# Score matmuls of two head pairs issued as one run of 24 on four PSUM banks

## The chip, the cores and the metric

One Trainium2 chip, one NeuronCore. The metric is the device time of the kernel in microseconds (us); lower is better. The engines that matter are TensorE (PE for its matmuls, PEld for its weight loads), VectorE (DVE), ScalarE (ACT), GpSimd (POOL) and SyncE (SP, whose queue starts most transfers).

## The reference

With DEPTH = 1 only the attention layer runs, then the final norm. S = 256 tokens, D = 1024, 16 heads of 64; the block of keys is 256 long, so every query attends causally inside the one block and nothing is gathered.

```
h = rms_norm(x, norm_g)
q, k, v, gate = split(h @ w_in, 4)
s_own = einsum('bhqd,bhld->bhql', q_c, k_own) * dh ** -0.5
s_own = s_own - slopes * (t_f[:, None] - pos_own[None, :])
s_own = where(pos_own[None, :] <= t_int[:, None], s_own, -inf)
p = softmax(s_own)
o = einsum('bhql,bhld->bhqd', p, v_own)
x = x + (o * silu(gate)) @ w_out
return rms_norm(x, final_norm_g)
```

## The kernel before

All matmuls work on fp32r operands that are split into a high and a low part, so that each product is three matmuls: high by high, high by low and low by high (lines 582, 650, 672). A weight piece of 128x1024 arrives by DMA as `w`, ACT copies it to `whi` (split_hi, line 230) and DVE subtracts to get `wlo` (split_lo, line 243); whi and wlo have four buffers each (NW), w has four (NL). split_lo also starts the next load on the SP queue.

The projections run part by part in the order of PARTS (line 28): v0 q0 k0 g0 q1 k1 g1 q2 k2 v1 q3 k3 g2 g3, each part accumulating in two of the eight PSUM banks (line 638). A q or k part j gives the transposed q or k of head pairs 2j and 2j+1. At a part's end `evac` (line 455) adds a small generator, a fiber, that scales the bank into z, splits it into hi and lo (qh, ql, kh, kl; lines 491 to 497) and, for a k part, adds a second fiber, `fiber_pair`, for each of the two pairs.

`fiber_pair(p)` (line 322) does the attention of heads 2p and 2p+1. It waits for q and k of its pair, takes two PSUM banks (one for each head), and issues 12 score matmuls (lines 344 to 349): for the second half of the queries (m = 1, 256 keys) and then for the first half (m = 0, 128 keys), three products, each for two heads. A head has 64 contraction rows, so the two heads use the upper and the lower 64 rows of the array and run as two at a time. Then DVE adds the ALiBi bias and takes the row extremes (line 365), ACT takes the exponentials with their sums (line 369), the rows are normalized (lines 375 to 389), TensorE transposes them (six transposes of 128x128, line 403, in `tr`, line 111), ACT and DVE split the transposed blocks into pth and ptl (lines 409 and 411), TensorE multiplies with v (lines 429 and 432), and cs, og, oh and ol (lines 437 to 453) give the output projection its operand: oh and ol of pair p are its k-step p.

The order of all queues is written out in advance. The program keeps a planner's clock for each engine (class Plan, line 64) and issues an instruction when the planner's time says that its inputs are there. After each projection matmul it calls `fill()`, which places weight splits by their due times, and `side()` (line 297), which lets the first ready fiber take one step up to its next `yield 0`. `poll()` looks again 50 ns later by the planner's clock. `take(keep)` (line 128) gives a bank only when more than `keep` banks are free; keep[0] is 2 during the projections, so that a pair takes its banks when four are free. `stage["s"]` counts the pairs whose scores are issued, `stage["t"]` those whose transposes are, and SWITCH = 100 ns is what the planner adds before and after each run of scores.

The output projection (line 670) uses five banks; k-steps 0 to 3 go through all of them, 15 matmuls each, and k-steps 4 to 7 then finish bank after bank (line 696), each finished bank going to the residual sum and the final norm (lines 700 to 718) and out.

Of the kernel before, what the change touches and what calls it, by code (L numbers as in the profile page):

```python
# [13 lines left out]
P = 128  # L14
S = 256
D = 1024
H = 16
DH = 64
# [30 lines left out]
NPR = 3  # L49
# [11 lines left out]
SWITCH = 100.0  # L61
# [26 lines left out]
def trunk(ctx: ExitStack, tc, laid, fin_g, out):  # L88
    nc = tc.nc
    plan = Plan()  # L90
# [37 lines left out]
    def take(keep):  # L128

        av = [b for b in banks if not b["busy"] and b["free"] <= plan.pe]  # L130
        if len(av) <= keep:
            return None
        b = min(av, key=lambda b: b["free"])
        b["busy"] = True
        return b

    def take_now():
        b = min((b for b in banks if not b["busy"]), key=lambda b: b["free"])
        b["busy"] = True
        return b  # L140
# [149 lines left out]
    at_q, at_k, at_v, at_g, at_o = {}, {}, {}, {}, {}  # L290
    qs, ks = {}, {}
    stage = {"s": 0, "t": 0, "v": 0, "e": 0}
    keep = [2]
# [25 lines left out]
    def poll():  # L319
        return plan.pe + 50.0  # L320

    def fiber_pair(p):
        while p not in at_k or p not in at_q:
            yield poll()
        qh, ql = qs[p]
        kh, kl = ks[p]
        yield max(at_k[p], at_q[p])
        while stage["s"] < p or stage["t"] < p - NPR + 1:
            yield poll()
        while True:  # L330
            b0 = take(keep[0] + 1)
            if b0 is not None:
                break
            yield poll()
        bs = [b0, take_now()]
        st = sp.tile([P, 2, P + S], F32, name="st")
        pr = sp.tile([P, 2, P + S], F32, name="pr")
        mx = sm.tile([P, 4], F32, name="mx")
        rs = sm.tile([P, 4], F32, name="rs")
        ri = sm.tile([P, 4], F32, name="ri")  # L340

        plan.pe += SWITCH
        at_s = {}
        for m, c in ((1, slice(0, S)), (0, slice(S, S + P))):
            for jj, (u, w) in enumerate(((qh, kh), (qh, kl), (ql, kh))):
                for a in range(2):
                    rr = slice(a * DH, (a + 1) * DH)
                    nc.tensor.matmul(bs[a]["t"][:, c], u[rr, m * P:(m + 1) * P], w[rr, 0:c.stop - c.start],  # L348
                                     start=jj == 0, stop=jj == 2)
                at_s[m] = plan.mm(c.stop - c.start)  # L350
        plan.pe += SWITCH
        stage["s"] = p + 1
        r = at_s[0]
        yield 0
        for m in (1, 0):
# [70 lines left out]
        for a in range(2):  # L426
            w = [vv[m][:, 2 * p + a].rearrange("p t n -> p (t n)") for m in range(NM)]
# [13 lines left out]
        for a in range(2):  # L441
            rr = slice(a * DH, (a + 1) * DH)
# [12 lines left out]
    def evac(kind, j, f, b, r):  # L455
        fibers.insert(0, [0.0, fiber_evac(kind, j, f, b, r)])
        if kind == "k":
            fibers.append([0.0, fiber_pair(2 * j + f)])
# [45 lines left out]
    with tc.manual_schedule():  # L504
# [132 lines left out]
        for kind, j in PARTS[1:]:  # L637
            acc = [take_now() for _ in range(2)]
            dep = [b["free"] for b in acc]
            w = CW if kind == "v" else GW  # L640
            kp = KP * GW // w
            for k in range(NK):
# [5 lines left out]
                for f in range(2):  # L648
                    fs = slice(f * P, (f + 1) * P)
                    for jj, (xx, ww) in enumerate(((xh, whi), (xl, whi), (xh, wlo))):  # L650
                        if kind == "v":
                            o, a, b = acc[f]["t"], xx[k][:, fs], ww[i][:, kk * w:(kk + 1) * w]
                        else:
                            o, a, b = acc[f]["t"][:, :S], ww[i][:, kk * w + f * P:kk * w + (f + 1) * P], xx[k]
# [33 lines left out]
        for m in range(NM):  # L688
# [4 lines left out]
            for u, (c0, c1) in enumerate(GROUPS[m]):  # L693
                c = slice(c0, c1)
# [63 lines left out]
```

## Time and profile before

| | |
|---|---|
| time, median of 3 runs | 147.12 us (146.87 to 147.26) |
| profiled execution, its own time | 147.17 us |
| its span, first to last instruction | 145.4 us |
| TensorE matmuls | 138.4 us busy, 95% of the span |
| TensorE weight loads | 126.8 us, 87% |
| VectorE | 119.8 us, 82% |
| ScalarE | 93.1 us, 64% |
| GpSimd | 13.6 us, 9% |
| mean granted TensorE clock | 0.989 of full |

The time is longer than the span by 1.77 us, which lie before the first and after the last instruction. Matmuls overlap one another in the record: the end of one is modelled, and what one costs in a stream is the distance from its start to the next start. A row of the timeline gives start and length in us, the engine, the source line, the operation, output and inputs, and the shapes; a bracket at its end is the idle time of the engine ahead of it and what ended it.

### The profile page before, as it was taken

What the parts mean: (1) busy time and instruction counts of PE and PEld (TensorE: products, weight loads), DVE (VectorE), ACT (ScalarE), POOL (GpSimd) and SP (SyncE); (2) the same over time, 40 slices, a digit from 0 to 9 for tenths busy, and PEclk for the clock granted to TensorE, in tenths of its full rate; (3) what the DMA queues carried; (4) which work ended last, traced back from release to release, by engine and by line L of the source; (5) the groups of instructions that cost most, each with busy time, mean ns of one, the idle gap of its engine ahead of it and who ended that gap; (6) DMA issues with size and microseconds to landing.
All of it is one profiled execution on the core that took longest, in us unless ns stands there. A gap on an engine that the chain in (4) does not pass through costs nothing.

```text
span 145.4 us, 2764 instructions
## 1 busy us (share of the span) xinstructions
PE 138.4 (95%) x1009; PEld 126.8 (87%) x1009; DVE 119.8 (82%) x291; ACT 93.1 (64%) x197; POOL 13.6 (9%) x29
## 2 busy tenths in 40 slices
PE   7999999999999999999999999999999999999930
PEld 5688899999999999999977789999899889888830
DVE  0999499888998996999999769877758999785870
ACT  3698977757976548976586867535596775531331
POOL 7891140000000000000000000000000000000210
PEclk9999999999999999999999999999999999999995
DMA  4999998596043264045476130875532134000123
GB/s 161 347 391 412 412 409 298 188 325 231 14 144 144 80 213 144 0 149 176 158 243 224 71 124 20 280 274 167 187 112 91 57 127 161 0 0 5 36 111 144
DMA packets 8078, 24.83 MB, mean 171 GB/s; under 512 B 896, under 2 KB 1408, under 8 KB 8064
## 3 DMA queue, kind: packets, MB, share of 16 engines
q1 hardware_dynamic: 7632, 23.73, 46.2%
q10 hardware_dynamic: 432, 0.92, 1.7%
q8 instruction: 8, 0.13, 0.4%
q14 instruction: 6, 0.05, 0.1%
HBM read 23.60 MB, written 1.05 MB: 170 GB/s over the span
## 4 chain that ended last, share of the span: by engine, by line
PE 89%; issue 3%; DMA 2%; DVE 1%; ACT 1%; POOL 1%; POOLq 0%
PE bank L107 81%; PE bank L348 5%; PE bank L111 4%; DMA w<-in_laid 2%; POOL fr L711 1%; DVE bias L702 1%; ACT bias L713 0%; POOLq L754 0%; DVE x L700 0%; ACT whi L118 0%; DVE fms L702 0%
## 5 line engine op out<-in xcount | busy, mean ns | idle before, releaser
L107 PE MATMUL bank<-xh,wlo 128*128 128x256 f32 x192 | 55.3, 288 | 0.0
L107 PE MATMUL bank<-xl,whi 128*128 128x256 f32 x192 | 55.1, 287 | 0.0
L107 PE MATMUL bank<-xh,whi 128*128 128x256 f32 x192 | 55.0, 287 | 0.0
L251 DVE TENSOR_TENSOR wlo<-w,whi 128x1024 fp32r<-128x1024 f32 (+1 forms) x43 | 48.9, 1142 | 6.7 <-ACT whi L118 6.7
L118 ACT ACTIVATE whi<-w 128x1024 fp32r<-128x1024 f32 (+1 forms) x43 | 41.8, 977 | 15.6 <-PE bank L107 7.9
L107 PEld LDWEIGHTS bank<-xh,whi 128*128 128x128 f32 x192 | 36.2, 189 | 0.3
L107 PEld LDWEIGHTS bank<-xh,wlo 128*128 128x128 f32 x192 | 36.2, 189 | 0.2
L107 PEld LDWEIGHTS bank<-xl,whi 128*128 128x128 f32 x192 | 36.2, 189 | 0.1
L118 ACT ACTIVATE pr<-st,mx 128x256 f32<-128x256 f32 (+1 forms) x32 | 14.1, 444 | 6.8 <-DVE mx L365 6.8
L107 PE MATMUL bank<-whi,ol 128*128 128x512 f32 (+1 forms) x35 | 12.7, 364 | 0.0
L711 POOL TENSOR_TENSOR fr<-fms,mhalf 128x1 f32<-128x1 f32 x2 | 1.6, 798 | 118.8 <-DVE fms L702 118.8
L107 PE MATMUL bank<-whi,oh 128*128 128x512 f32 (+1 forms) x35 | 12.7, 362 | 0.0
L107 PE MATMUL bank<-wlo,oh 128*128 128x512 f32 (+1 forms) x35 | 12.6, 359 | 0.0
L107 PE MATMUL bank<-whi,xh 128*128 128x512 f32 x32 | 12.3, 427 | 0.1
L111 PE MATMUL bank<-ident,pr 128*128 128x128 f32 x48 | 12.1, 272 | 0.0
L482 DVE TENSOR_TENSOR z<-bank,rows 128x256 f32<-128x256 f32 x24 | 9.4, 420 | 2.7 <-PE bank L107 2.6
L107 PE MATMUL bank<-whi,xl 128*128 128x512 f32 x32 | 11.6, 403 | 0.0
L107 PE MATMUL bank<-wlo,xh 128*128 128x512 f32 x32 | 11.6, 401 | 0.0
L118 ACT ACTIVATE pth<-bank 128x384 fp32r<-128x384 f32 x16 | 7.9, 492 | 4.1 <-PE bank L111 3.8
L365 DVE CUSTOM_DVE_ANT_0 st<-bank,bias 128x256 f32<-128x256 f32 (+1 forms) x32 | 9.8, 352 | 0.2 <-PE bank L348 0.2
L411 DVE TENSOR_TENSOR ptl<-bank,pth 128x384 fp32r<-128x384 f32 x16 | 8.8, 552 | 1.1 <-ACT pth L118 1.1
L107 PE MATMUL bank<-ptl,vv 128*128 128x256 f32 (+1 forms) x32 | 8.9, 278 | 0.0
(81 smaller groups left out, 210.1 us busy)
## 6 DMA issues: line engine op xcount, KB each, us to landing
w<-in_laid SPq DMA_DIRECT2D x36, 512.0 KB, 4.1
w<-in_laid SPq DMA_DIRECT2D x7, 256.0 KB, 5.0
x<-in_laid SPq DMA_DIRECT2D x2, 512.0 KB, 6.8
head<-in_laid SPq DMA_DIRECT2D x3, 256.0 KB, 5.1
out<-bias SPq DMA_DIRECT2D x2, 320.0 KB, 2.3
gf<-in_fin_g ACTq DMA_DIRECT2D x1, 512.0 KB, 5.5
out<-bias SPq DMA_DIRECT2D x2, 192.0 KB, 1.9
w<-in_laid ACTq DMA_DIRECT2D x1, 256.0 KB, 3.1
```

What stands on the lines that cost most here:

```text
L107: nc.tensor.matmul(o, a, b, start=start, stop=stop)
L111: nc.tensor.transpose(o, a, ident)
L118: nc.scalar.activation(o, i, fn, scale=scale, **kw)
L251: nc.vector.tensor_sub(wlo[i][:, c], w32[i][:, c], f32(whi[i][:, c]))
L348: nc.tensor.matmul(bs[a]["t"][:, c], u[rr, m * P:(m + 1) * P], w[rr, 0:c.stop - c.start], start=jj == 0, stop=jj == 2)
L365: nc.vector.tensor_tensor_reduce(st[:, a, c0:c1], ps, bt, scale=-1.0, scalar=BIG, op0=ALU.add, op1=ALU.min, accum_out=mx[:, cc:cc + 1])
L411: nc.vector.tensor_sub(lo[:, a], pv, f32(hi[:, a]))
L482: nc.vector.tensor_mul(z, ps, rows8 if kind == "q" else rows)
L702: nc.vector.tensor_tensor_reduce(sq[:, :c1 - c0], y[:, c], y[:, c], scale=1.0 / D, scalar=ms[:, u - 1:u], op0=ALU.mult, op1=ALU.add, accum ...
L711: nc.gpsimd.tensor_tensor(r, ms[:, ns - 1:ns], mhalf, op=ALU.pow)
```

## The change

The scores move out of fiber_pair into a new generator, scores(p), which the fiber of each even pair p runs for the pairs p and p+1. It waits until q and k of both pairs are there, takes four banks (it asks for more than keep[0] + 3, that is six free ones during the projections), and issues 24 matmuls without a yield: the second query half of pair p, that of pair p+1, the first query half of p, that of p+1. The planner's SWITCH is added twice for 24 matmuls. The fiber of an odd pair waits until stage["s"] has passed it. The wait on stage["t"], which guards the three st and pr buffers, comes behind the scores. Everything from line 355 on is unchanged.

```
+    def scores(p):
+        while not all(u in at_k and u in at_q for u in (p, p + 1)):
+            yield poll()
+        yield max(t[u] for t in (at_k, at_q) for u in (p, p + 1))
+        while stage["s"] < p:
+            yield poll()
...
-            b0 = take(keep[0] + 1)
+            b0 = take(keep[0] + 3)
...
-        bs = [b0, take_now()]
+        both = [b0] + [take_now() for _ in range(3)]
+        plan.pe += SWITCH
+        for u in (p, p + 1):
+            of_pair[u] = both[2 * (u - p):2 * (u - p) + 2], {}
+        for m, c in ((1, slice(0, S)), (0, slice(S, S + P))):
+            for u in (p, p + 1):
+                bs, at_s = of_pair[u]
+                (qh, ql), (kh, kl) = qs[u], ks[u]
+                for jj, (q, k) in enumerate(((qh, kh), (qh, kl), (ql, kh))):
+                    for a in range(2):
+                        rr = slice(a * DH, (a + 1) * DH)
+                        nc.tensor.matmul(bs[a]["t"][:, c], q[rr, m * P:(m + 1) * P], k[rr, 0:c.stop - c.start],
+                                         start=jj == 0, stop=jj == 2)
+                    at_s[m] = plan.mm(c.stop - c.start)
+        plan.pe += SWITCH
+        stage["s"] = p + 2
+        yield 0
+
+    def fiber_pair(p):
+        if p % 2 == 0:
+            yield from scores(p)
+        while stage["s"] <= p:
+            yield poll()
+        bs, at_s = of_pair.pop(p)
+        while stage["t"] < p - NPR + 1:
+            yield poll()
...
-        plan.pe += SWITCH
-        at_s = {}
-        for m, c in ((1, slice(0, S)), (0, slice(S, S + P))):
-            for jj, (u, w) in enumerate(((qh, kh), (qh, kl), (ql, kh))):
-                for a in range(2):
-                    rr = slice(a * DH, (a + 1) * DH)
-                    nc.tensor.matmul(bs[a]["t"][:, c], u[rr, m * P:(m + 1) * P], w[rr, 0:c.stop - c.start],
-                                     start=jj == 0, stop=jj == 2)
-                at_s[m] = plan.mm(c.stop - c.start)
-        plan.pe += SWITCH
-        stage["s"] = p + 1
```

## Rows read from the trace of the kernel before

**Rows 1.** The page, part 1: engine, busy us, share of span, instructions.
```profile
PE 138.4 (95%) x1009; PEld 126.8 (87%) x1009; DVE 119.8 (82%) x291; ACT 93.1 (64%) x197; POOL 13.6 (9%) x29
```

**Rows 2.** Waits: who waited for whom, us in total, times, longest.
```profile
PEld bank L107 <- ACT whi L118: 0.8, 1, 0.8
...
PEld bank L348 <- issue: 0.7, 2, 0.4
```

**Rows 3.** The chain that ended last: by line, then pieces (start, us, what).
```profile
by line: PE bank L107 80.7%; PE bank L348 4.6%; PE bank L111 3.8%; issue 3.1%; DMA w<-in_laid 2.1%; POOL fr L711 0.6%; DVE bias L702 0.5%; ACT bias L713 0.5%; POOLq L754 0.5%; DVE x L700 0.5%; ACT whi L118 0.4%; DVE fms L702 0.0%
...
75.56 0.84 PE bank L348 x12
76.39 0.90 PE bank L107 x3
...
120.45 13.45 PE bank L107 x73
```

**Rows 4.** Windows over two score groups: length, busy us of each engine, clock, DMA.
```profile
31.30:33.72 2.42, 2.42 (x30) 2.01 (x28) 1.77 (x5) 0.79 (x2) 0.00 (x0) 1.00 0.91 320
...
75.16:78.39 3.23, 3.23 (x30) 2.31 (x29) 3.20 (x9) 1.66 (x3) 0.00 (x0) 1.00 0.65 223
```

**Rows 5.** Timeline of TensorE's matmuls around the scores of pairs 0 and 1.
```profile
31.30 0.28 PE L107 MATMUL bank<-xl,whi 128*128 128x256 f32 x1
31.51 0.39 PE L348 MATMUL bank<-kh,qh 64*128 64x256 f32 x2
31.73 0.28 PE L348 MATMUL bank<-kl,qh 64*128 64x256 f32 x2
31.85 0.28 PE L348 MATMUL bank<-kh,ql 64*128 64x256 f32 x2
31.96 0.23 PE L348 MATMUL bank<-kh,qh 64*128 64x128 f32 x2
32.02 0.28 PE L348 MATMUL bank<-kl,qh 64*128 64x128 f32 x2
32.13 0.28 PE L348 MATMUL bank<-kh,ql 64*128 64x128 f32 x2
32.34 0.39 PE L107 MATMUL bank<-xh,wlo 128*128 128x256 f32 x1
...
33.49 0.38 PE L107 MATMUL bank<-xh,whi 128*128 128x256 f32 x1
33.72 0.28 PE L107 MATMUL bank<-xl,whi 128*128 128x256 f32 x1
33.83 0.28 PE L107 MATMUL bank<-xh,wlo 128*128 128x256 f32 x1
```

**Rows 6.** Timeline of VectorE: the last kl of a group, and a reduction that waited.
```profile
30.64 0.75 DVE L495 TENSOR_TENSOR kl<-z,kh 128x256 fp32r<-128x256 f32 x2
...
55.19 0.42 DVE L365 CUSTOM_DVE_ANT_0 st<-bank,bias 128x256 f32<-128x256 f32 x1 [0.15 <-PE bank L348]
...
75.71 0.42 DVE L495 TENSOR_TENSOR kl<-z,kh 128x256 fp32r<-128x256 f32 x1
```

**Rows 7.** Timeline of TensorE: last scores of pair 3, and three later matmuls.
```profile
54.88 0.28 PE L348 MATMUL bank<-kh,ql 64*128 64x128 f32 x2
...
93.10 0.28 PE L107 MATMUL bank<-xh,wlo 128*128 128x256 f32 x1
...
125.03 0.28 PE L107 MATMUL bank<-ptl,vv 128*128 128x128 f32 x1
...
130.70 0.39 PE L107 MATMUL bank<-xh,ol 128*128 128x512 f32 x1
```

**Rows 8.** Timeline of VectorE: two weight splits, and the last ol.
```profile
88.75 1.22 DVE L251 TENSOR_TENSOR wlo<-w,whi 128x1024 fp32r<-128x1024 f32 x1
...
127.56 1.22 DVE L251 TENSOR_TENSOR wlo<-w,whi 128x1024 fp32r<-128x1024 f32 x1
...
129.83 0.42 DVE L452 TENSOR_TENSOR ol<-og,oh 128x256 fp32r<-128x256 f32 x1
```

More of the change, by code (lines that the diff above doesn't have):

```diff
@@ L320, in poll @@
         return plan.pe + 50.0
-    def fiber_pair(p):
-        while p not in at_k or p not in at_q:
+    of_pair = {}
+    def scores(p):
+        while not all(u in at_k and u in at_q for u in (p, p + 1)):
             yield poll()
[L325 to L328, printed above, removed]
+        yield max(t[u] for t in (at_k, at_q) for u in (p, p + 1))
+        while stage["s"] < p:
             yield poll()
         while True:
-            b0 = take(keep[0] + 1)
+            b0 = take(keep[0] + 3)
             if b0 is not None:
```

## The prediction

> **What bounds the kernel now.** I read the busy shares first: TensorE's matmuls fill 138.4 us of the span, and no other engine is above 82% [rows 1]. A busy matmul is only a hint, so the list of waits comes next: what TensorE waits for by name is over before the projections are under way (0.8 us for the first whi), and from then on the only idle time on its side is 0.7 us ahead of two runs of scores, ended by "issue", that is by nothing another engine did [rows 2]. The chain that ended last says the same: line 107 has 80.7%, the scores' line 348 has 4.6% and the transposes' line 111 has 3.8%, together 89%, and it runs on TensorE without a break, the last piece being 73 matmuls from 120.45 to 133.9 us [rows 3]. So TensorE's own stream is the path, and a microsecond taken out of it should move the end by a microsecond, as long as nothing that feeds it becomes late. The granted clock is 1.00 in both score groups shown [rows 4], the upper of its two levels, so the clock is no part of the cost here.
>
> Then I look at what a run of scores costs in that stream [rows 5], by distances between starts. Undisturbed, a projection matmul of 256 columns follows the last by 0.12 us (33.72 to 33.83). Four distances around a run of scores are longer: from the last projection matmul into the run 0.21 (31.30 to 31.51), first to second score 0.22 (31.51 to 31.73), from the last score out 0.21 (32.13 to 32.34), and first to second projection matmul after it 0.23 (33.49 to 33.72). So entering and leaving costs 0.09 + 0.10 + 0.09 + 0.11 = 0.39 us, while the scores inside follow one another at 0.11 to 0.12, but for one short step of 0.06 where the columns go from 256 to 128. There are eight runs, in four groups of two; three groups have one projection matmul between the two runs, the third has three (0.90 us) [rows 3].
>
> **The change part by part.** Removed: four of the eight runs' entries and exits. The 96 score matmuls and their weight loads stay: 12 in each of eight runs, or six steps of two, since the two heads go side by side. Given back: a run of 24 has one short step of 0.06 where two runs of 12 have two, so each merge loses 0.12 − 0.06, about 0.05. Per merge 0.39 − 0.05 = 0.34. I check it on the whole stretch: from 31.30 to 33.72 are 2.42 us [rows 4], with three projection matmuls (0.35) and 12 steps of two scores (12 by 0.115 = 1.38) in them; the remaining 0.69 is two entries and exits, net of the short steps, so 0.35 each. The third group has projection matmuls of 512 columns, and its distances are longer than normal by the same amounts. I take 0.35 by 4 = 1.40 us. Bounds for one merge: 0.40 if the second short step is kept (the whole 0.39, rounded up), and 0.25 if the first score of the second pair still pays its 0.10, which no row of before can show, as there no score of another pair follows a score; the nearest row is the step from one query half to the next in the same run (31.85 to 31.96), which costs nothing extra, so I stay at 0.35. That is 1.0 to 1.6 us for four.
>
> The Trainium skill has the mechanism as a rule: "TensorEngine Tiling (Array Packing)", Key Properties, says that changing the tiling mode, and not merely the tile, drains the engine. "TensorE: Matmul & The Clock Gate", Single matmul latency, puts a lone warm matmul at (398 + N)/2.4 ns, 272 ns for 256 columns; as an estimate from these two pages a drain would cost 0.272 − 0.118 = 0.154 us and eight mode changes saved 1.23 us. The trace's own distances give 1.40, and I keep those.
>
> Moved: only TensorE's instructions; the diff issues no transfer and no work on another engine. In three groups the second pair's 12 matmuls go ahead of one projection matmul. In the third group it is the other way round: pair 5's kl ends at 76.13 [rows 6], while pair 4's scores ran from 75.5 [rows 3, 4], so the merged run can't stand before about 76.2, and more likely stands where pair 5's run stood, 1.7 us later than pair 4's did. In the first group the last kl ends at 31.39 [rows 6], before the run of pair 0 at 31.51, so nothing is held up. Behind the run on TensorE's queue stand projection matmuls, which wait for nothing else.
>
> Added wait one, the banks: six free instead of four. The second run of each group before was issued when four banks were free besides the two of the accumulating part and the two that the first pair had just taken; that is the same six. As the second run followed within 1.2 to 1.7 us each time [rows 3, 5], the new condition is met by then. Cost: none for the stream, since projection matmuls fill the time; if it were never met the scores would wait for a whole part, which is the slow rival below.
>
> Added wait two, the softmax: a reduction on line 365 waits for the last score matmul in its bank, not for its own columns: the one at 55.19 was released by the scores that end at 54.88 + 0.28 = 55.16 [rows 6, 7], although its own half was issued earlier. In the new order pair p's banks are complete after 18 of 24 matmuls, about 0.2 us later than after 12 of 12, and pair p+1's some 0.6 earlier. In the third group pair 4's softmax starts about 2 us later. The cover is the projection matmuls that TensorE does meanwhile; VectorE's part of the pair stays the same work. I cost it at nothing; uncovered it would be at most those 2 us, once.
>
> The Trainium skill's "PSUM — Partial Sum Buffer", section on bank collisions, says that two engines may not touch one bank on the same partitions at once, whichever columns they use. The wait at 55.19 agrees with it. By that page the new order works against the change: if VectorE's reductions were on the path, pair p's 0.2 us would be paid in each of four groups, 0.8 in all, and the sum would be 0.6 us. The waits of TensorE [rows 2] show none for them.
>
> **Who is late next.** Weights have room: the tightest wlo after the first scores that I found ends at 89.97 and is first used at 93.10 [rows 7, 8], 3.1 us, and its pace follows TensorE's release of the buffers. The tight place is the end. The last ol is done at 130.25 [rows 8] and used at 130.70 [rows 7]: 0.45 us. But its chain starts from pair 7's last product with v at 125.03 [rows 7], a TensorE instruction behind all scores, so a rigid shift takes it along and the 0.45 stays.
>
> **Sum.** 147.17 − 1.40 = 145.77 for an execution like the profiled one. The median of the runs is 0.05 lower than that execution, so 145.7.
>
> **The rivals.** *Partly eaten at the end.* The planner's clock loses only 0.2 us per merge (two SWITCH) where the chip loses 0.35, and its choices downstream can change. If one more split of 1.22 us [rows 8] comes to stand ahead of the last ol, TensorE waits 1.22 − 0.45 = 0.77 and the gain is 0.63: 146.5. For it: three VectorE steps already queue there back to back. Against: the splits' number is fixed. *The runs don't get cheaper, or the gain is all lost.* If what costs is the change of pair and bank and not the change of row mode, each merge saves only about half, 0.7 us in all, and one wait of 0.77 as above eats it: 147.17 − 0.70 + 0.77 = 147.2. Against: the undisturbed half-to-half step. *Slower.* Pair 7's product with v falls behind one more k-step of the output projection: 15 matmuls at 13.45/73 = 0.184 us [rows 3], 2.8 us. TensorE then waits 2.8 − 0.45 = 2.35 at the first use of the last ol, 147.17 − 1.40 + 2.35 = 148.1. It decides once that product is later by 1.40 + 0.45 = 1.85 us against the matmuls that follow; the delay of the third group's softmax shows how such a delay arises, but pairs 4 and 5 aren't the last ones, and for pairs 6 and 7 q and k come long enough together.
>
> **How the numbers follow.** A difference of about 0.3%, 0.44 us, is what the measurement can tell from none. Forecast, 145.2 to 146.2: 0.66. Partly eaten, 146.2 to 146.7: 0.11. No net change: 0.10. Slower: 0.13. Faster by over 0.3% therefore 0.77, same 0.10, slower 0.13. The range takes in the bounds 1.0 to 1.6 and the partly eaten case, and reaches a little into the third: 145.2 to 147.0.
>
> **What would show it.** In the profile after, four runs of 24 matmuls, each with one entry and one exit, about 1.95 us (2.42 − 0.35 − 0.12) from the projection matmul ahead of it to the second one behind it; in the third group a later start. Right, if TensorE still has no named wait, and the distance between the first scores and the last projection matmul shrinks by 1.4. Wrong, if the step from pair to pair inside a run is 0.2, or if TensorE shows a wait for ol, xl, pth or pr; then the loss is that wait.

## The result, and the profile after

The changed kernel takes 146.66 us (median of 10 runs, 146.01 to 146.91) against 147.34 for the kernel before in the same comparison (10 runs, 146.87 to 147.68): a ratio of 0.9946, 95% interval 0.9929 to 0.9964. It is faster by 0.5%, about half of what was forecast. (The ratio is not the quotient of the two medians, which is 0.9954 here; further down the two differ by up to 0.24%.) The execution that was profiled took 146.18 us with a span of 144.4 us, 0.99 us less than the profiled execution before.

The runs of scores first. The chain of the changed kernel (start, length in us, what) has four runs of 24 where that of the kernel before has eight of 12 (one of them in [rows 3]), and the windows over the first and the third group (length, then busy time of PE, PEld, DVE, ACT and POOL, granted clock, DMA share, GB/s) answer to [rows 4]:

```profile
31.80 1.53 PE bank L348 x24
53.02 1.53 PE bank L348 x24
76.57 1.53 PE bank L348 x24
101.12 1.53 PE bank L348 x24
```

```profile
31.52:33.49 1.97, 1.97 (x29) 1.76 (x27) 1.58 (x4) 0.36 (x1) 0.00 (x0) 1.00 0.96 360
76.18:78.37 2.19, 2.19 (x27) 1.75 (x26) 1.91 (x5) 0.10 (x1) 0.00 (x0) 1.00 0.54 204
```

The first stretch goes from the last projection matmul ahead of the scores to the second one behind them; before it was 2.42 us with one projection matmul more in it, so a merge saves 2.42 − 0.12 − 1.97 = 0.33 us. In the third group it is 3.23 − 3 by 0.233 − 2.19 = 0.34, since three projection matmuls of 512 columns more stood in the stretch before. The timeline of the first run shows one entry, one exit, and no extra distance at the step from pair to pair (32.07 to 32.19, 32.71 to 32.82):

```profile
31.52 0.28 PE L107 MATMUL bank<-xl,whi 128*128 128x256 f32 x1
31.73 0.39 PE L348 MATMUL bank<-kh,qh 64*128 64x256 f32 x2
31.96 0.28 PE L348 MATMUL bank<-kl,qh 64*128 64x256 f32 x2
32.07 0.28 PE L348 MATMUL bank<-kh,ql 64*128 64x256 f32 x2
32.19 0.29 PE L348 MATMUL bank<-kh,qh 64*128 64x256 f32 x2
...
32.71 0.29 PE L348 MATMUL bank<-kh,ql 64*128 64x128 f32 x2
32.82 0.29 PE L348 MATMUL bank<-kh,qh 64*128 64x128 f32 x2
...
33.05 0.29 PE L348 MATMUL bank<-kh,ql 64*128 64x128 f32 x2
33.27 0.38 PE L107 MATMUL bank<-xh,wlo 128*128 128x256 f32 x1
33.49 0.28 PE L107 MATMUL bank<-xh,whi 128*128 128x256 f32 x1
```

Now what is new. Behind the scores the list of waits has idle time on TensorE's side that [rows 2] had not (a wait of 0.4 us for a wlo is new as well, but it lies at 7.2 us, in the beginning):

```profile
PEld bank L107 <- ACT oh L118: 0.6, 1, 0.6
...
PEld bank L107 <- DVE ol L467: 0.2, 1, 0.2
```

TensorE waits for the last pair's oh and ol. Its timeline there, and VectorE's and ScalarE's (compare [rows 7, 8]):

```profile
128.59 0.39 PE L107 MATMUL bank<-whi,ol 128*128 128x512 f32 x1
129.13 0.50 PE L107 MATMUL bank<-xh,oh 128*128 128x512 f32 x1
129.47 0.40 PE L107 MATMUL bank<-xl,oh 128*128 128x512 f32 x1
129.71 0.39 PE L107 MATMUL bank<-xh,ol 128*128 128x512 f32 x1
```

```profile
126.19 0.85 DVE L458 TENSOR_TENSOR og<-bank,cs 64x256 f32<-64x256 f32 x2
127.07 1.23 DVE L251 TENSOR_TENSOR xl<-w,xh 128x1024 fp32r<-128x1024 f32 x1
128.22 0.42 DVE L462 TENSOR_TENSOR og<-og,head 128x256 f32<-128x256 f32 x1
129.12 0.42 DVE L467 TENSOR_TENSOR ol<-og,oh 128x256 fp32r<-128x256 f32 x1 [0.48 <-ACT oh L118]
```

```profile
124.50 1.05 ACT L118 ACTIVATE xh<-w 128x1024 fp32r<-128x1024 f32 x1
125.57 0.59 ACT L118 ACTIVATE cs<-bank 64x512 f32<-64x512 f32 x1
128.66 0.42 ACT L118 ACTIVATE oh<-og 128x256 fp32r<-128x256 f32 x1 [2.50 <-DVE og L462]
```

The steps from 128.59 to 129.13 and to 129.47 are 0.54 and 0.34 us where an undisturbed one is 0.23: 0.42 us lost. The last weight split, xl, stands on VectorE's queue between the last pair's og sum (line 458) and its og product (line 462). Before, the product stood ahead of both last splits, the wlo at 127.56 of [rows 8] and xl:

```profile
126.84 0.43 DVE L447 TENSOR_TENSOR og<-og,head 128x256 f32<-128x256 f32 x1
...
128.69 1.22 DVE L251 TENSOR_TENSOR xl<-w,xh 128x1024 fp32r<-128x1024 f32 x1
```

TensorE's path falls into three stretches that can be read from the starts of its matmuls in each timeline: from the first matmul of g0's second piece (30.82 before) to the first output matmul; from there to the last matmul of k-step 3; from there to the last matmul of all. They leave out the beginning, which differs between executions. Each line is one profiled execution; the changed kernel and e1 are the same program and differ by 0.19 us in the first stretch, in three small steps at which no wait is named, so a difference of up to 0.2 us there tells nothing about the programs. The last stretch of the two agrees to 0.02.

| kernel | to first output matmul | k-steps 0 to 3 | to last matmul | total |
|---|---|---|---|---|
| before | 82.85 | 14.34 | 11.25 | 108.44 |
| changed | 81.58 | 14.33 | 11.67 | 107.58 |
| e1, changed again | 81.77 | 14.34 | 11.69 | 107.80 |
| e2, split after product | 81.60 | 14.33 | 11.25 | 107.18 |
| e3, cs ahead of xh | 81.59 | 14.33 | 11.54 | 107.46 |
| e4, both moves | 81.60 | 14.34 | 11.25 | 107.19 |
| e5, full matmul inside | 83.36 | 14.34 | 11.25 | 108.95 |
| e6, full matmul ahead | 81.86 | 14.35 | 11.25 | 107.46 |
| e7, pair after pair | 81.92 | 14.34 | 11.25 | 107.51 |
| e8, no hold of the last pair | 81.92 | 14.00 | 11.26 | 107.18 |

So the stream got 1.27 us shorter and the end took 0.42 back: 0.86 us in all, and the remaining 0.13 of the 0.99 between the two profiled executions is an earlier start (30.69 against 30.82).

### The profile page after: what moved, and what is told of

Read it like the earlier page. It is cut to its first block, busy times and chain, and to the rows that moved or that the text cites. A ratio compares the mean times of both kernels' runs of the same rounds, so it can differ in the third digit from the quotient of the medians.

```text
span 144.4 us, 2760 instructions
## 1 busy us (share of the span) xinstructions
PE 137.2 (95%) x1009; PEld 126.0 (87%) x1009; DVE 119.5 (83%) x291; ACT 92.1 (64%) x197; POOL 13.6 (9%) x29
## 4 chain that ended last, share of the span: by engine, by line
PE 84%; issue 4%; ACT 3%; DVE 3%; DMA 2%; POOL 1%; POOLq 0%
PE bank L107 76%; PE bank L348 4%; PE bank L111 4%; DMA w<-in_laid 2%; ACT whi L118 1%; DVE xl L251 1%; ACT xh L118 1%; POOL fr L726 1%; DVE og L458 1%; DVE bias L717 1%; ACT oh L118 1%; ACT bias L728 1%; POOLq L769 0%; DVE x L715 0%; ACT cs L118 0%
## 5 line engine op out<-in xcount | busy, mean ns | idle before, releaser
L107 PE MATMUL bank<-whi,xh 128*128 128x512 f32 x32 | 11.7, 407 | 0.2 <-ACT whi L118 0.2
```

The costliest lines, as they stand in the source:

```text
L107: nc.tensor.matmul(o, a, b, start=start, stop=stop)
```

## The experiments

The theory after the result: the merges save what the distances say, and the loss is made by the order of the tail, one split ahead of the last og product ("end order"). Rivals: the merges saved less than computed ("stream"), the last pair's products with v come too late with ScalarE's cs behind xh ("late product with v"), and for the saving itself, that it is the interruption that costs and not the row mode.

**e1, the changed kernel again**, on the same chip as the next three.

> The changed kernel once more, to stand beside the three below on one chip. Theory 'end order': TensorE's stream is 1.40 us shorter up to the output projection, and 0.4 us (as in its first profile) or more is lost at the first use of the last pair's oh, because VectorE does the last weight split xl (1.23 us) between the last pair's og sum and og product. It should read 0.7 to 1.0 us under the kernel before, with idle time of TensorE released by the last oh. Theory 'stream': the runs of scores themselves saved less than 0.35 us each; then no such idle time is needed to explain the result, and the distance between the first scores and the first output matmul shrank by less than 1.4.

146.37 us (7 runs, 146.09 to 146.65) against 147.23 for the kernel before, ratio 0.9918 (0.9886 to 0.9949): 0.86 us less. The wait for oh is there again, 0.6 us in the list, and the tail is 11.69 us, as "end order" said. The first stretch shrank by 1.08 here and by 1.27 in the first profile, both under the 1.40 of the sum, so "stream" isn't refuted by this run alone; a small part of it is in fact true, as no profile of the changed kernel reached 1.40.

**e2, the last split behind the last product.**

```
+    scaled = []
...
-            if i < nsplit[0]:
+            if i < nsplit[0] and (i < N_PIECES - 1 or scaled):
...
         d = dve(S, max(d, at_g[p]))
+        if p == NP - 1:
+            scaled.append(d)
```

One instruction moves on VectorE; the orders of TensorE and ScalarE stay as in the changed kernel.

> The changed kernel with one instruction moved: on VectorE the last weight split xl stands behind the last pair's og product instead of ahead of it; TensorE's and ScalarE's orders are untouched. Theory 'end order': the last oh comes 1.2 us sooner, ahead of TensorE, so the whole 1.40 us shows: 0.4 us or more faster than the changed kernel on the same chip, about 1.4 us under the kernel before (ratio about 0.990), no idle time of TensorE released by oh. Theory 'late product with v' (the last pair's products with v were themselves put too late, and ScalarE's cs behind xh): the chain stays late and less than 0.2 us comes back. Theory 'stream': equal to the changed kernel.

145.81 us (5 runs, 145.60 to 146.03), ratio 0.9891 (0.9861 to 0.9920): 1.42 us under the kernel before and 0.56 under e1, and the times of the two don't overlap. In the stretches e2 is 1.26 under the kernel before and 0.62 under e1, 0.44 of it in the tail. VectorE's and TensorE's timelines of e2:

```profile
126.22 0.85 DVE L459 TENSOR_TENSOR og<-bank,cs 64x256 f32<-64x256 f32 x2
127.10 0.42 DVE L463 TENSOR_TENSOR og<-og,head 128x256 f32<-128x256 f32 x1
127.44 1.22 DVE L251 TENSOR_TENSOR xl<-w,xh 128x1024 fp32r<-128x1024 f32 x1
128.58 0.42 DVE L470 TENSOR_TENSOR ol<-og,oh 128x256 fp32r<-128x256 f32 x1
```

```profile
128.61 0.39 PE L107 MATMUL bank<-whi,ol 128*128 128x512 f32 x1
128.84 0.39 PE L107 MATMUL bank<-xh,oh 128*128 128x512 f32 x1
129.07 0.40 PE L107 MATMUL bank<-xl,oh 128*128 128x512 f32 x1
129.31 0.40 PE L107 MATMUL bank<-xh,ol 128*128 128x512 f32 x1
```

The product comes at 127.10 and not at 128.22, every step of TensorE is 0.23, and the tail is 11.25 us as before the change. So the whole 0.42 was the place of that one split. The same og sum at the same time (126.22, 126.19) shows that nothing upstream was moved.

**e3, cs ahead of xh.**

```
+    copied = []
...
-            if i < N_PIECES and i < used[0] + (NW if i < N_PIECES - 1 else NW + 1) and i in w_at:
+            if i < N_PIECES and (i < N_PIECES - 1 or copied) and i < used[0] + (NW if i < N_PIECES - 1 else NW + 1) and i in w_at:
...
         e = act(cs, po[DH:P], AF.Copy, 2 * S, r, True)
+        if p == NP - 1:
+            copied.append(e)
```

> The changed kernel with one instruction moved on ScalarE: the last pair's cs copy stands ahead of the last weight copy xh instead of behind it; TensorE's and VectorE's orders are untouched. Theory 'end order': cs is 0.35 us sooner, but xl now waits for the later xh (about 126.9 by the first profile's times) and still stands ahead of the og product, so only about 0.15 us comes back. Theory 'late product with v': the 0.35 us come back, nearly all of the 0.4. Theory 'stream': equal to the changed kernel.

146.30 us (12 runs), ratio 0.9933 (0.9912 to 0.9954). Its median is only 0.07 us under e1's, so the time says little. The tail is 11.54 us, 0.13 under the changed kernel's, as "end order" said (0.15), and not the 0.35 of "late product with v". VectorE's queue shows why: xl is still ahead of the product, at 127.19.

```profile
127.19 1.23 DVE L251 TENSOR_TENSOR xl<-w,xh 128x1024 fp32r<-128x1024 f32 x1
128.33 0.42 DVE L465 TENSOR_TENSOR og<-og,head 128x256 f32<-128x256 f32 x1
```

**e4, both moves.**

> Both moves of the two runs before together. Theory 'end order': xh is later by the cs copy, xl waits for it and not for the product, about 126.9 + 1.2 = 128.1 to 128.7, still ahead of its use at 129.06: the same time as with the first move alone, about 1.4 us under the kernel before. Theory 'late product with v': better than either move alone by 0.2 us or more.

The trace has e2's stretches to 0.02 us, as expected of "end order". The time is 146.16 us (12 runs, 145.58 to 147.47), ratio 0.9925 (0.9898 to 0.9953); its executions spread so widely that the time alone wouldn't tell e4 from e2 or e3.

**e5 and e6, what a run of scores costs.** To e2's kernel one more matmul, of 128 rows and 128 columns, is added for each run, in e5 between the two halves, in e6 ahead of the run. It computes nothing that is used. The order of the other matmuls is e2's in both. The code shown is e5's; in e6 the same matmul stands ahead of the first line shown. e5 to e8 ran on another chip than e1 to e4, so they are set beside e2 by the stretches.

```
         for m, c in ((1, slice(0, S)), (0, slice(S, S + P))):
+            if m == 0:
+                nc.tensor.matmul(of_pair[p][0][0]["t"][:, S + P:], xh[0][:, :P], xh[0][:, :P], start=True, stop=True)
             for u in (p, p + 1):
```

> The second run's kernel (xl behind the last og product) with one extra matmul in each of the four runs of scores: 128 rows by 128 columns of xh against xh, written to columns of a score bank that nothing reads, between the 12 scores of the second query halves and the 12 of the first. It adds work that the reference doesn't have. Theory 'row mode' (what a run costs beyond its scores is the step from 128 rows to 64 and back): each extra matmul costs its own 0.12 us and a way out and in, 0.33 to 0.35 us, so four cost 1.8 to 1.9 us: the stretch from the first g0 matmul of the second piece to the first output matmul is 1.8 us longer than in the second run. Theory 'interruption' (what was saved is not the mode but the projection matmul, the planner's steps or the waits around a run): four cost 0.5 us.

> As the run before, but each extra matmul stands ahead of its run of scores, next to a projection matmul, so that no row mode changes. Both theories: 0.12 us each, 0.5 us for the four, against the second run. 'Row mode': 1.3 us less than the run before. 'Interruption': equal to the run before.

e5 takes 147.68 us (10 runs), ratio 1.0023 (0.9996 to 1.0051): all of the gain is gone with four matmuls of 128 rows put into the runs. e6 takes 146.52 us (10 runs), ratio 0.9938 (0.9910 to 0.9967). The same four matmuls make the first stretch 1.76 us longer inside the runs and 0.26 us longer ahead of them. The chain of e5, and then that of e6, in the first group:

```profile
31.88 0.91 PE bank L351 x12
32.79 0.26 PE bank L344
33.05 0.81 PE bank L351 x12
```

```profile
33.04 0.06 PE bank L342
33.10 1.53 PE bank L350 x21
```

A matmul that costs 0.06 us beside its like costs 0.26 + 0.91 + 0.81 − 1.53 = 0.45 between scores. So the step from 128 rows to 64 and back is what a run pays for, 1.76 − 0.26 = 1.50 us for four; "interruption" is refuted. Without its own 0.06 such a matmul costs 0.39, the very sum of the four distances that the prediction read. e6's 0.26 was under the expected 0.5: behind the extra matmul, with its 128 columns, the distance into the run is 0.15 us instead of 0.21.

**e7, pair after pair.**

```
-        for m, c in ((1, slice(0, S)), (0, slice(S, S + P))):
-            for u in (p, p + 1):
+        for u in (p, p + 1):
+            for m, c in ((1, slice(0, S)), (0, slice(S, S + P))):
```

> The second run's kernel with the 24 scores in another order: all 12 of pair p, then all 12 of pair p+1. Each run then has two short steps of 0.06 us (256 to 128 columns) where the changed kernel has one: the run takes 1.48 and not 1.53 us, 0.2 us less for four, if a change of pair and bank in the row mode costs nothing. If it does cost (the 0.10 us of the first score of a run), the order of the changed kernel, with three changes of pair against one, is the dearer one by 0.2 more for each run. Time: 0.2 us under the second run, about 0.988 of the kernel before; or equal, where the end takes it back.

145.93 us (12 runs, 145.48 to 147.30), ratio 0.9917 (0.9894 to 0.9940): no better than e2. The expectation of 0.2 us was wrong; the time could hardly have shown it (the intervals of e2 and e7 overlap), but the trace does. The timeline of its second run shows the second short step (55.00 to 55.06), and that the way back from 128 to 256 columns costs what it gives (54.59 to 54.76, 0.17 instead of 0.115):

```profile
54.59 0.33 PE L349 MATMUL bank<-kh,qh 64*128 64x256 f32 x2
54.76 0.28 PE L349 MATMUL bank<-kl,qh 64*128 64x256 f32 x2
...
55.00 0.23 PE L349 MATMUL bank<-kh,qh 64*128 64x128 f32 x2
55.06 0.27 PE L349 MATMUL bank<-kl,qh 64*128 64x128 f32 x2
```

That run is 1.51 us against 1.53. The change from pair to pair costs nothing, 0.11 (54.48 to 54.59). In the first group of this profile the run also waited 0.2 us for a kl and took 1.77 us; that makes up most of the 0.32 that its first stretch has over e2's. It isn't the added wait of the change: the second step of the run, which uses pair 0's own kl, starts at 32.65, right behind the end of the first of the two kl (32.18 + 0.42 = 32.60), so pair 0 alone would have waited too.

**e8, where the order of the tail comes from.** In the changed kernel seven of the eight reductions of pairs 6 and 7 stand together and the eighth far behind:

```profile
105.42 0.28 DVE L380 CUSTOM_DVE_ANT_0 st<-bank,bias 128x128 f32<-128x128 f32 x1
...
108.94 0.84 DVE L458 TENSOR_TENSOR og<-bank,cs 64x256 f32<-64x256 f32 x2
...
109.89 0.28 DVE L380 CUSTOM_DVE_ANT_0 st<-bank,bias 128x128 f32<-128x128 f32 x1
```

In the kernel before, the last of the eight came ahead of the next og sum:

```profile
106.91 0.28 DVE L365 CUSTOM_DVE_ANT_0 st<-bank,bias 128x128 f32<-128x128 f32 x1
...
110.50 0.84 DVE L443 TENSOR_TENSOR og<-bank,cs 64x256 f32<-64x256 f32 x2
```

The planner holds a reduction back while ScalarE or VectorE is planned more than 1 us ahead of TensorE. e8 takes this rule away for pair 7 alone:

```
-                while plan.t["act"] > plan.pe + BACK or plan.t["dve"] > plan.pe + BACK:
+                while p < NP - 1 and (plan.t["act"] > plan.pe + BACK or plan.t["dve"] > plan.pe + BACK):
                     yield poll()
```

> The changed kernel without the planner's rule that a reduction waits while ScalarE or VectorE is planned more than 1 us ahead of TensorE, for the last pair alone. In the changed kernel this rule put the last pair's last reduction 4 us behind the other seven, its last transpose behind the products of pair 6 with v, and its own products with v six matmuls later. Theory 'cause of the order is the held reduction': without the rule the tail has the order of the kernel before (og product, then the two weight splits), TensorE has no idle time released by the last oh, and the time is that of the second run, about 0.990 of the kernel before. Theory 'tail order is only chance': TensorE waits somewhere else at the end, 0.3 us or more, and the time stays near that of the changed kernel.

145.90 us (6 runs, 145.73 to 146.59), ratio 0.9912 (0.9883 to 0.9941). The total of the stretches is e2's, 107.18 us; 0.34 of it moved from the second stretch to the first, because three of the last transposes (line 111) now stand ahead of the first output matmul, 9 behind it where all other kernels of the table have 12. TensorE waits for no oh, and VectorE ends as in the kernel before, product, then splits:

```profile
125.44 0.43 DVE L462 TENSOR_TENSOR og<-og,head 128x256 f32<-128x256 f32 x1
...
126.16 1.22 DVE L251 TENSOR_TENSOR wlo<-w,whi 128x1024 fp32r<-128x1024 f32 x1
127.29 1.22 DVE L251 TENSOR_TENSOR xl<-w,xh 128x1024 fp32r<-128x1024 f32 x1
```

So the order of the tail came from one reduction of 0.28 us that the 1 us rule held back: with the rule, pair 7 runs late and the last split gets ahead of its product; without it, the loss is gone. Here the order and the stretches decide, not the time, since e8's ratio (0.9912) is hardly under e1's (0.9918), though their medians are 0.47 us apart. Why the planner's clocks crossed that limit only with the merged scores was not followed further; that is left open, and so is whether other small changes of the plan would have removed the loss as well.

## Why the prediction was right or wrong

*What bounds the kernel:* right. The first stretch is free of named waits after the beginning, and what left TensorE's stream left the time: e2, which differs from the changed kernel in the place of one instruction, is 1.26 us under the kernel before in the stretches and 1.42 between the medians.

*Price of an entry and exit:* right in kind and 5 to 10% too high. Forecast 0.35 us for a merge, read 0.33 and 0.34 in the windows, 1.25 to 1.27 us over the first stretch in four of the five profiles with this order (e1: 1.08) against 1.40. This took 0.13 from the gain. Its bounds of 1.0 to 1.6 hold, and the worry that the second pair's first score pays again is settled: 0.115 us.

The drain rule of "TensorEngine Tiling (Array Packing)", Key Properties, which the prediction cited from the Trainium skill, agrees with e5: one 128-row matmul costs 0.45 us between 64-row scores and 0.06 beside its like. That the engine drains meanwhile is not seen in a trace. The estimate that the prediction made from pages of the Trainium skill, 1.23 us, came nearer to the 1.27 than the 1.40 did; no run here tests its price for a single drain, so that is no proof of it.

*Added wait one, banks:* right; the merged runs stand where the later of the two runs stood, in the third group at 76.50 us, where pair 5's run before, less the two savings ahead of it and the earlier start, gives 77.22 − 0.66 − 0.13 = 76.43. *Added wait two, softmax:* costed at nothing. As a wait this was right: TensorE shows none for a reduction, pth or pr. Two readings in it were wrong: pair 0's last score step starts 0.98 us into the run (31.73 to 32.71) against 0.62 before (31.51 to 32.13), so 0.36 later and not 0.2, and pair 1's 1.32 against 1.78, 0.46 earlier and not 0.6. They cost nothing. What the item left out is that the planner may answer a softmax by another order, as it did when it let the last reduction slip.

*Who is late next:* this is the step that failed. The prediction found the right place, the end with its 0.45 us, and then argued that the chain starts behind all scores, so that "a rigid shift takes it along and the 0.45 stays". The shift is not rigid, since each queue's order is made anew by the planner's clocks. What the runs showed in its place: TensorE waits for the last pair's oh and ol and loses 0.42 us, because one split of 1.22 us came to stand ahead of the last og product, and the loss is gone when that split (e2) or the planner's hold of the last reduction (e8) is moved out of the way. The rival "partly eaten at the end" named this kind of loss and was given a chance of 0.11. Its place was another: it put one more split ahead of the last ol, but both last splits stood ahead of ol already in the kernel before (127.56 and 128.69 against 129.83); new is the split ahead of the product, and so of oh. Its price was put at 0.77 and measured at 0.42. That its gain, 0.63 us, is near the 0.68 between the medians is luck: it is 1.40 − 0.77, and the stretches show 1.27 − 0.42.

*The numbers:* 146.66 lies in 145.2 to 147.0, and faster by over 0.3% came true. Of the 1.40 us forecast, 0.13 were missing in the merges and 0.42 were lost at the end; the last 0.17 down to the 0.68 between the medians is less than the 0.35 by which the medians of e2 and e4 differ, whose stretches are alike. The forecast of 145.7 is near the time of a kernel without the loss at the end, e2 with 145.81, e8 with 145.90 and e4 with 146.16, though those save 1.26 us in the stretches and not 1.40.

## What to carry to other kernels

A change of the TensorE row mode is paid on entry and on exit, 0.33 to 0.39 us for a run here, so small matmuls of one mode belong in one run, where other work can wait for it. Where an order is made by a planner, a saving on one engine is a new input to every later choice: before counting on slack at the end, find out which work may come to stand ahead of the last user, and pin that order by a condition. A loss at the end can be found by comparing the two orders of the last few instructions on each queue, and proved by moving one of them.

## What the runs showed that was not expected

In the row mode a step from 128 columns back to 256 costs 0.17 us instead of 0.115, just what the step of 0.06 from 256 to 128 had gained (e7).

Executions of one kernel differ by 0.5 us and more, and much of it lies at the beginning, ahead of everything the change touches: the first matmul of g0's second piece starts between 30.68 us (e8) and 31.94 us (e6), with TensorE waiting there for the first weights; the lists of waits of the changed kernel and then of e6 show 0.7 us of it. The stretches of the table are therefore the better measure of a few tenths, down to the 0.2 us by which the first of them differs in one program.

```profile
PEld bank L107 <- ACT whi L118: 0.9, 1, 0.9
```

```profile
PEld bank L107 <- ACT whi L118: 1.6, 2, 0.9
```
